# Attention output turned by VectorE in 32 by 32 blocks, and put together by the reload, in place of TensorE transposes

## The chip, the cores and the metric

The kernel runs on one core of one Trainium2 chip. The metric is the device time of one execution in microseconds (us), and the median of the runs is compared. A core has five engines that run their own instruction lists side by side: TensorE (PE, matmuls, with its weight loads as PEld), VectorE (DVE), ScalarE (ACT), GpSimd (POOL) and SyncE (SP), which here issues the DMA transfers, in the order of its list. Engines wait for each other by semaphores. On-chip tiles have 128 partitions (rows of SBUF); PSUM holds the results of PE.

## The reference

One layer of a bidirectional hybrid encoder, for 1024 tokens of width 1024, in float32. What bears on the change:

```python
h = rmsnorm(x, norm_mix)
q, k, v, r, lr_f, lr_b, u, g_a, g_b = split(h @ w_in)      # one wide projection
# 4 heads of 128 key and 256 value columns, chunks of the sequence, both directions
o = o_fwd + o_bwd
o = o * rsqrt(mean(o * o, axis=-1) + 1e-6)                   # per token and head
o = o.transpose(0, 2, 1, 3).reshape(1, 1024, 1024) * gla_norm
o = o * silu(r)
y_a = o @ w_branch_gla
# y_b: pooled mixer of u; merged = sigmoid(g_a) * y_a + sigmoid(g_b) * y_b
x = x + merged @ w_out
# then a SwiGLU feed-forward block with a residual, and a last rmsnorm
```

The attention output `o` comes out with tokens on the partitions. The gate `r` is computed with its columns on the partitions and tokens along the free axis. The product `o * silu(r)` needs both in one layout, the second, and that is where the change sits.

## The kernel before, in words

**Precision.** Matmuls take each float32 operand as a rounded high part and a remainder, and make three products (high x high, low x high, high x low). ACT makes the high part (`wh`, `trh`; helper line L200, or L718), and VectorE or GpSimd subtracts it for the low part (`wl`, `trl`; L201, L709). So a weight that comes from HBM passes DMA, then ACT, then GpSimd, before PE can use it. All matmuls are recorded at one line, L279.

**Stages.** The q and k columns of the projection are made by PE with the attention of the four heads woven in between, from about 130 to 310 us. After the last of them stands a loop over six columns of `r`, 128 wide each: `for j in range(KT - 2)` (L1223; KT is 8). Column j takes its weights (`raw`, two loads of 256 KB at L208, issued ahead), and for each of two halves of 512 tokens runs 24 matmuls (`feature_major`). The r columns 0 to 2 are put aside; from j = 3 on, each half first handles one that was put aside (`put_by`) and then its own, both by `gated`.

**`gated(j, half, src)`** (L1193 on). ACT computes Silu of the r half into `sr` (L1196). PE turns four 128x128 pieces of the attention output `o_heads` into a PSUM bank `tp` (L1199). VectorE multiplies `tp`, `sr` and the norm's factor into a tile `o` (L1206). When two columns are done, both halves are stored to `ob_out` (at a later step, by `flush`, L574). Columns 6 and 7 of r come out of the first gate unit below and pass `gated` there.

**Gate units.** After the loop, pairs of columns are computed together by a scheme of seven products in place of eight (`Gates.run`). Unit 0 holds r columns 6 and 7 and runs products 1, 2, 6, 5, 3, 7. Its weights are `fraw` (512 KB per column, L1096), from which VectorE makes sums `fs` (L1104). Product 1 and 2 use tiles that are on the chip. Product 6 is the first that uses a sum of blocks of the activations: such sums were written to HBM earlier (`f_out`), are loaded into `hs` (L684), and become `trh` on ACT (L718) and `trl` on VectorE (L709). Product 6 also needs a PSUM bank that ACT empties by a copy into `ga` (L1492). There are three `hs` tiles in turn, so a load of `hs` waits for the `trl` of the one three before it. On ACT, the casts `trh`, the Silus, the casts `wh` and the copies `ga` stand in one list.

**The attention output's way.** A head's output is held in two tiles `o` of 128x1024: half of the tokens each, 4 groups of 128 tokens by 256 value columns. `normalize` (L1030) scales the eight groups by 1/rms on VectorE. For heads 0 to 2 both tiles are then stored to `o_out` in HBM (L574), and `load_o` brings them back as `ol` at j = 2, 3 and 4 of the loop (L1044, two loads of 512 KB a head). Head 3, which ends right before column j = 3's first transposes, stays in SBUF.

**What sets the order.** The program is written out by generators: `pump` moves the attention's steps on beside PE's matmuls, `beside` moves the `hs` loads and casts on, `soon` puts a step off by a number of steps. What results is a fixed list for each engine. SP's list is one line for all loads and stores above: an instruction in it that waits holds up all behind it. Eight semaphores serve SP's transfers in rotation, so a transfer also waits for the landing of the one eight places before it.

Of the kernel before, what the change touches and what calls it, by code (L numbers as in the profile page):

```python
# [10 lines left out]
F32 = mybir.dt.float32  # L11
# [4 lines left out]
ALU = mybir.AluOpType  # L16

P = 128
# [3 lines left out]
NT = SEQ // P  # L22
HALF = 512
HEADS = 4
DK = 128
DV = 256
RANK = 16
CH = 128
SUB = 64
GROUPS = 4  # L30
WINDOWS = (2, 4, 8, 16)
# [22 lines left out]
def kernel(  # L54
# [20 lines left out]
    nc = tc.nc  # L75
# [10 lines left out]
    ps_g = ctx.enter_context(tc.tile_pool(name="ps_g", bufs=8 - MM_BANKS, space=bass.MemoryType.PSUM))  # L86

    dram = ctx.enter_context(tc.tile_pool(name="dram", bufs=1, space=bass.MemoryType.DRAM))
# [4 lines left out]
    def name(s):  # L93
        count[0] += 1
        return f"{s}_{count[0]}"

    def slot(dtype=F32, shape=(2, HALF), s="slot"):
        return slots.tile([P, *shape], dtype, tag="slot", name=name(s))

    def t2(width=HALF, dtype=F32, s="t"):  # L100
        return tmp.tile([P, width], dtype, tag="t2", name=name(s), padded_shape=[P, HALF + 2 * PAD])
# [4 lines left out]
    def vec(width, s="v"):  # L106
        return small.tile([P, width], F32, tag="vec", name=name(s), bufs=12)

    def bank(pool, s="ps"):
        return pool.tile([P, HALF], F32, tag=pool.name, name=name(s))  # L110
# [5 lines left out]
    ident = const.tile([P, P], F32, tag="ident", name="ident")  # L116
# [8 lines left out]
    keep = const.tile([P, 4, P], U8, tag="keep", name="keep")  # L125
    carry = const.tile([P, HALF // SUB, SUB], BF16, tag="carry", name="carry")

# [26 lines left out]
    def soon(delay, *steps):  # L154
        put_off.extend([delay, step] for step in steps)
# [36 lines left out]
    def finish_side():  # L192
        while side:
            for _ in side[0][0]:
                pass
            side.pop(0)
# [61 lines left out]
    def take(ahead=True):  # L258

        if not ready:  # L260
            prepare()
        w = ready.pop(0)
        w.finish()
        if ahead:
            prepare()
        return w
# [3 lines left out]
    def halves(ap):  # L270
        return ap.rearrange("p (a c) -> p a c", a=2)

    def sorted_(ap):

        return ap.rearrange("p (c a) -> p a c", a=2)
# [37 lines left out]
    def rms_scale(ms, width, s):  # L313
        rs = vec(width, s)
        nc.vector.tensor_scalar(rs[:, :], ms, EPS, None, op0=ALU.add)
        nc.gpsimd.tensor_tensor(rs[:, :], rs[:, :], half_neg[:, :width], op=ALU.pow)
        return rs
# [132 lines left out]
    g_mix, g_ffn, g_gla, g_pool = (cols[:, 8 * i : 8 * i + 8] for i in range(4))  # L450
    b_dec = (cols[:, 32:36], cols[:, 36:40])
    HALVES = slice(0, HALF), slice(HALF, D)
# [116 lines left out]
    def later(dst, src):  # L569
        deferred.append((dst, src))  # L570
# [105 lines left out]
    def feature_parts():  # L676
        todo = [(p, c) for p in (6, 5, 7, 4) for c in range(2)]
        wholes = []

        def load_sum():  # L680
            if len(wholes) < len(todo):
                p, c = todo[len(wholes)]
                wholes.append(slot(s="hs"))
                nc.sync.dma_start(wholes[-1][:, :, :], f_out[p][:, c])  # L684

        yield load_sum, None, None
        for n, (p, c) in enumerate(todo):
            yield load_sum, wholes[n][:, :, :], p
# [46 lines left out]
    def prepare_beside(jobs, every, put=PUT, lag=1):  # L735
        aside.append([beside(chain(*jobs), every, put, lag), every])

    def finish_beside():
        while aside:
            for _ in aside[0][0]:  # L740
                pass
            aside.pop(0)


    o_heads, unscaled = {}, []
# [78 lines left out]
    def attention(h):  # L824
# [28 lines left out]
        def decay(half, d):  # L853
# [3 lines left out]
            tot = vec(8, "tot")  # L857
            cs3 = cs.rearrange("p (n c) -> p n c", c=SUB)
            la3 = la.rearrange("p (n c) -> p n c", c=SUB)
            cy = carry.rearrange("p n c -> p (n c)")  # L860
            if d == 0:
                nc.vector.tensor_tensor_scan(cs[:, :], cy, la[:, :], 0.0, op0=ALU.mult, op1=ALU.add)
                nc.vector.tensor_copy(tot[:, :], cs3[:, :, SUB - 1])
            else:
# [4 lines left out]
                )  # L869
                nc.vector.tensor_tensor(tot[:, :], cs3[:, :, SUB - 1], la3[:, :, SUB - 1], op=ALU.add)  # L870
            first = cs.rearrange("p (n a c) -> p n a c", a=2, c=SUB)[:, :, 0, :]
            tot2 = tot.rearrange("p (n a) -> p n a", a=2)
# [31 lines left out]
        def chunk_of(e, n, d):  # L904
            return e[n // 4][:, d, (n % 4) * CH : (n % 4 + 1) * CH]

# [28 lines left out]
        def scores(half):  # L935
            sc = [bank(ps_g, "sc") for _ in range(2)]
            for d in range(2):
                for i in range(4):
                    n = 4 * half + i
                    nc.tensor.matmul(  # L940
                        sc[d][:, i * CH : (i + 1) * CH], chunk_of(ke, n, d), chunk_of(qe, n, d),
                        start=True, stop=True,
                    )
            hi, lo = (t2(dtype=F32R, s="p")[:, :] for _ in range(2))
            nc.vector.copy_predicated(sc[1][:, :], keep.rearrange("p n c -> p (n c)"), sc[0][:, :])
            split_to(hi, lo, sc[1][:, :])
            return hi, lo
# [41 lines left out]
        p = scores(0)  # L989
# [3 lines left out]
        o = [slot(shape=(4, DV), s="o") for _ in range(2)]  # L993
        ms = vec(NT, "oms")
        old = sf = None
        for n in range(NT):
            half, i = n // 4, n % 4
# [22 lines left out]
            if n == 3:  # L1020
                p = q_next
            yield 1.02
        rs = rms_scale(ms[:, :], NT, "ors")
        if h == HEADS - 1:
            o_heads[h] = o

        def normalize():
            for n in range(NT):
                t = o[n // 4][:, n % 4, :]
                nc.vector.tensor_scalar(t, t, rs[:, n : n + 1], None, op0=ALU.mult)  # L1030
            if h < HEADS - 1:
                for half in range(2):
                    later(o_out[h][:, 4 * half : 4 * half + 4, :], o[half][:, :, :])

        unscaled.append(normalize)
        if h == HEADS - 1:
            unscaled.pop()()

    o_out = [dram.tile([P, NT, DV], F32, name=f"o_out{h}") for h in range(HEADS - 1)]

    def load_o(h):
        o_heads[h] = [slot(shape=(4, DV), s="ol") for _ in range(2)]
        for half in range(2):
            nc.sync.dma_start(o_heads[h][half][:, :, :], o_out[h][:, 4 * half : 4 * half + 4, :])  # L1044

    def sums_behind():
        prepare_beside(map(feature_sums, range(2)), 2)
# [145 lines left out]
    def gated(j, half, src):  # L1193

        sr = t2(s="sr")
        nc.scalar.activation(halves(sr[:, :]), src, AF.Silu)  # L1196
        tp = bank(ps_g, "tp")
        for i in range(4):
            nc.tensor.transpose(  # L1199
                tp[:, i * P : (i + 1) * P],  # L1200
                o_heads[j // 2][half][:, i, (j % 2) * P : (j % 2 + 1) * P], ident[:, :],
            )
        if j // 2 not in oT:
            oT[j // 2] = [slot(s="o") for _ in range(2)], []
        tiles, there = oT[j // 2]
        nc.vector.scalar_tensor_tensor(  # L1206
            tiles[half][:, j % 2, :], tp[:, :], g_gla[:, j : j + 1], sr[:, :], op0=ALU.mult, op1=ALU.mult
        )
        there.append((j, half))
        if len(there) == 4:  # L1210
            c = j // 2 % 2
            for half, t in enumerate(tiles):
                later(ob_out[j // 4, half][:, 2 * c : 2 * c + 2, :], t[:, :, :])
            soon(2, flush)
# [6 lines left out]
    BY = 3  # L1221
    sums_begun = False
    for j in range(KT - 2):  # L1223
        if 2 <= j <= 4:
            load_o(j - 2)
        w = take()
        if j == 4:
            for _ in range(2):
                gunits[0].load()
        if j == 5:  # L1230
            gates_ahead.step()
        if j < BY:
            whole_r = slot(s="r")
        for half in range(2):
            if j >= BY and not sums_begun and (j > BY or not side):
                finish_side()
                finish_beside()
                prepare_beside([feature_parts()], 5)
                sums_begun = True
            ps = feature_major(w, hT, half)  # L1240
            if half == 0:
                flush()
            elif j == KT - 3:
                for _ in range(2):
                    gunits[1].load()
            if j < BY:
                nc.scalar.copy(halves(whole_r[:, half, :]), sorted_(ps[:, :]))
                raw_r.append((j, half, halves(whole_r[:, half, :])))
            else:
                put_by()  # L1250
                gated(j, half, sorted_(ps[:, :]))
            if j == KT - 3 and half == 0:
                gates_ahead.step()
# [833 lines left out]
    for at, p in enumerate(OUT_ORDER):  # L2087
# [9 lines left out]
        for i in range(CLOSE if closing else n_of):  # L2097
            n = at * n_of + i
# [57 lines left out]
```

## Time and profile before

| | us |
|---|---|
| median of 3 runs (lowest to highest) | 1325.27 (1325.08 to 1325.62) |
| the profiled execution | 1323.53 |
| its span, first to last instruction | 1321.8 |
| PE busy | 1302.2 (99% of the span) |
| VectorE busy | 838.3 (63%) |
| ACT busy | 645.3 (49%) |
| GpSimd busy | 769.0 (58%) |
| transposes at L1199 | 64, from 310.9 to 370.6 |
| stores to `o_out` at L574 | 6, from 131.3 to 257.6 |
| reloads at L1044 | 6, from 260.7 to 302.3 |

Rows of the profile start with a time from the span's start where they come from the timeline (start, length, engine, line, operation, tile written <- tiles read, shape, and in brackets how long the engine was idle before and what released it). Rows by line give the count, the shortest, median and longest duration in ns, and the first and last start. Matmuls overlap on PE, so the distance of their starts is their cost, not their length. For SP, "SPq" marks the issue of a transfer, not the transfer; rows named DMA count the packets that moved in a window of time.

### The profile page before, as it was taken

Reading aid. Unit: us, or ns where it says so; the run is one execution under the profiler, and the core shown is the slowest. Engines: PE = TensorE matmul, PEld = TensorE weight load, DVE = VectorE, ACT = ScalarE, POOL = GpSimd, SP = SyncE. Lnnn points to the kernel's source line nnn. Section 1 sums busy time; section 2 is a strip of 40 time slices with the busy share of each in tenths; the row PEclk is TensorE's granted clock in tenths of the full one; section 3 lists DMA queues with packets and bytes.
Section 4 is the critical chain, followed back from the end, with each engine's and each line's share of the span. In section 5 each row is a group of like instructions: output and inputs, shape, how many; then the busy total and the mean of one; then the engine's idle time right before and its main releaser. Section 6 shows DMA issues by size and latency. Waiting matters only on the chain. (4 is left out here: it accounts for less than half of the span.)

```text
span 1321.8 us, 17901 instructions
## 1 busy us (share of the span) xinstructions
PE 1302.2 (99%) x6310; PEld 1138.0 (86%) x6310; DVE 838.3 (63%) x1034; ACT 645.3 (49%) x1177; POOL 769.0 (58%) x557
## 2 busy tenths in 40 slices
PE   9999999999999999999999999999999999999998
PEld 7888888899888888888888888888888888888886
DVE  6975556554735876778884856566666657354375
ACT  7366766665534545554347633333333334454353
POOL 3332734132598657669675286777766778465454
PEclk9999999999999999999999999999999999999999
DMA  7231623134778678996516355555444457995562
GB/s 236 104 104 42 198 75 117 59 101 128 239 247 283 195 223 303 380 409 212 185 65 240 127 189 186 183 183 173 155 142 159 150 160 257 382 349 201 182 223 80
DMA packets 167835, 251.97 MB, mean 191 GB/s; under 512 B 11161, under 2 KB 94145, under 8 KB 167745
## 3 DMA queue, kind: packets, MB, share of 16 engines
q1 hardware_dynamic: 167600, 250.57, 55.8%
q8 instruction: 49, 0.80, 0.3%
q14 instruction: 42, 0.34, 0.1%
q10 hardware_dynamic: 144, 0.26, 0.1%
HBM read 168.74 MB, written 82.05 MB: 190 GB/s over the span
## 5 line engine op out<-in xcount | busy, mean ns | idle before, releaser
L201 POOL TENSOR_TENSOR wl<-fs,wh 128x512 fp32r<-128x512 f32 x124 | 190.7, 1543 | 138.8 <-ACT wh L200 80.9
L279 PE MATMUL ps<-gh,wh 128*128 128x512 f32 x616 | 234.4, 381 | 0.5 <-DVE sums L1880 0.3
L279 PE MATMUL ps<-gl,wh 128*128 128x512 f32 x616 | 233.6, 379 | 0.7 <-DVE gl L1713 0.7
L279 PE MATMUL ps<-gh,wl 128*128 128x512 f32 x616 | 233.5, 379 | 0.0
L201 POOL TENSOR_TENSOR wl<-fraw,wh 128x512 fp32r<-128x512 f32 x93 | 131.1, 1410 | 58.0 <-ACT wh L200 52.8
L201 POOL TENSOR_TENSOR ol<-gor,oh 128x1024 fp32r<-128x1024 f32 (+1 forms) x42 | 103.2, 2462 | 76.0 <-ACT oh L200 63.1
L279 PE MATMUL ps<-hh,wh 128*128 128x512 f32 x356 | 141.1, 396 | 0.7 <-ACT ga L1492 0.7
L279 PE MATMUL ps<-hh,wl 128*128 128x512 f32 x356 | 134.9, 379 | 0.0
L279 PE MATMUL ps<-hl,wh 128*128 128x512 f32 x356 | 134.9, 379 | 0.0
L279 PEld LDWEIGHTS ps<-gh,wh 128*128 128x128 f32 x616 | 116.5, 189 | 17.9 <-DVE sums L1880 0.7
L279 PEld LDWEIGHTS ps<-gl,wh 128*128 128x128 f32 x616 | 116.4, 189 | 17.4 <-DVE gl L1713 1.1
L279 PEld LDWEIGHTS ps<-gh,wl 128*128 128x128 f32 x616 | 116.4, 189 | 16.5
L279 PE MATMUL ps<-oh,oh 128*128 128x512 f32 x308 | 116.8, 379 | 0.2 <-DVE g L1886 0.2
L279 PE MATMUL ps<-ol,oh 128*128 128x512 f32 x308 | 116.7, 379 | 0.0
L279 PE MATMUL ps<-oh,ol 128*128 128x512 f32 x308 | 116.7, 379 | 0.0
L201 POOL TENSOR_TENSOR wl<-wraw,wh 128x512 fp32r<-128x512 f32 x56 | 91.4, 1663 | 38.3 <-ACT wh L200 36.2
L201 POOL TENSOR_TENSOR wl<-raw,wh 128x512 fp32r<-128x512 f32 x34 | 47.0, 1392 | 103.2 <-ACT wh L200 70.3
L201 DVE TENSOR_TENSOR ol<-wor,oh 128x1024 fp32r<-128x1024 f32 (+1 forms) x42 | 66.6, 1601 | 62.6 <-ACT oh L200 55.1
L200 ACT CAST wh<-fs 128x512 fp32r<-128x512 f32 x124 | 75.8, 612 | 25.7 <-DVE fs L1104 23.8
L279 PEld LDWEIGHTS ps<-hh,wl 128*128 128x128 f32 x356 | 67.3, 189 | 9.6
L279 PEld LDWEIGHTS ps<-hh,wh 128*128 128x128 f32 x356 | 67.4, 189 | 9.3 <-ACT ga L1492 1.1
L279 PEld LDWEIGHTS ps<-hl,wh 128*128 128x128 f32 x356 | 67.4, 189 | 8.4
(281 smaller groups left out, 3059.4 us busy)
## 6 DMA issues: line engine op xcount, KB each, us to landing
fraw<-in_w_ffn_in_dram SPq DMA_DIRECT2D x44, 512.0 KB, 5.9
gor<-g_out SPq DMA_DIRECT2D x35, 512.0 KB, 5.7
fraw<-in_w_in_dram SPq DMA_DIRECT2D x22, 512.0 KB, 6.1
g_out<-s SPq DMA_DIRECT2D x44, 256.0 KB, 2.4
wor<-t_out SPq DMA_DIRECT2D x20, 512.0 KB, 4.2
raw<-in_w_in_dram SPq DMA_DIRECT2D x36, 256.0 KB, 5.2
g_out<-g SPq DMA_DIRECT2D x33, 256.0 KB, 2.6
x<-in_x_dram SPq DMA_DIRECT2D x16, 512.0 KB, 5.2
```

Of the source, the lines that this page charges most:

```text
L200: nc.scalar.copy(hi, src)
L201: eng.tensor_tensor(lo, src, as_f32(hi), op=ALU.subtract)
L279: nc.tensor.matmul(ps.rearrange("p (c a) -> p c a", a=2), a, b.rearrange("p (a c) -> p c a", a=2), **flags)
```

## The change: how heads are turned

The transposes on PE go. VectorE turns each 32x32 block of a head's tile in place, right after the normalisation of that half. All four heads are stored to `o_out` now, head 3 too, half by half. A block turned by itself has its columns on the right rows within 32, but lies in the wrong place of the 128x128 piece. The reload puts it right: for each of the two value columns groups of a head, four DMAs gather 32 value columns of all tokens onto 32 partitions, in pieces of 32 floats (128 bytes). A head's reload is 8 DMAs of 32x32x32 elements in place of 2 of 128x1024, and it now runs for j = 2 to 5. `gated` reads the result straight from SBUF.

```diff
+TB = 32
...
-        if h == HEADS - 1:
-            o_heads[h] = o
 
         def normalize():
-            for n in range(NT):
-                t = o[n // 4][:, n % 4, :]
-                nc.vector.tensor_scalar(t, t, rs[:, n : n + 1], None, op0=ALU.mult)
-            if h < HEADS - 1:
-                for half in range(2):
-                    later(o_out[h][:, 4 * half : 4 * half + 4, :], o[half][:, :, :])
+            for half, t in enumerate(o):
+                for i in range(4):
+                    n = 4 * half + i
+                    nc.vector.tensor_scalar(t[:, i, :], t[:, i, :], rs[:, n : n + 1], None, op0=ALU.mult)
+                turn_blocks(t[:, :, :].rearrange("p n c -> p (n c)"))
+                later(o_out[h][:, 4 * half : 4 * half + 4, :], t[:, :, :])
...
-    o_out = [dram.tile([P, NT, DV], F32, name=f"o_out{h}") for h in range(HEADS - 1)]
+    o_out = [dram.tile([P, NT, DV], F32, name=f"o_out{h}") for h in range(HEADS)]
+
+    def turn_blocks(ap, src=None):
+        nc.vector.transpose(ap, ap if src is None else src)
 
     def load_o(h):
-        o_heads[h] = [slot(shape=(4, DV), s="ol") for _ in range(2)]
-        for half in range(2):
-            nc.sync.dma_start(o_heads[h][half][:, :, :], o_out[h][:, 4 * half : 4 * half + 4, :])
+
+        for i in range(2):
+            t = slot(shape=(NT, P // TB, TB), s="ol")
+            for b in range(P // TB):
+                c = i * P + b * TB
+                nc.sync.dma_start(
+                    t[b * TB : (b + 1) * TB, :, :, :],
+                    o_out[h][:, :, c : c + TB].rearrange("(a p) n c -> p n a c", p=TB),
+                )
+            o_heads[2 * h + i] = t[:, :, :, :].rearrange("p n a c -> p (n a c)")
...
-        tp = bank(ps_g, "tp")
-        for i in range(4):
-            nc.tensor.transpose(
-                tp[:, i * P : (i + 1) * P],
-                o_heads[j // 2][half][:, i, (j % 2) * P : (j % 2 + 1) * P], ident[:, :],
-            )
...
-            tiles[half][:, j % 2, :], tp[:, :], g_gla[:, j : j + 1], sr[:, :], op0=ALU.mult, op1=ALU.mult
+            tiles[half][:, j % 2, :], o_heads[j][:, HALVES[half]], g_gla[:, j : j + 1], sr[:, :], op0=ALU.mult, op1=ALU.mult
...
     for j in range(KT - 2):
-        if 2 <= j <= 4:
+        if 2 <= j <= 5:
             load_o(j - 2)
```

The engines' lists move as follows. Lines are those of each kernel's own file, and numbers after a name tell apart the tiles of one name.

First VectorE, from the 1/rms of head 3 to the first gated products, before the change:

```order
L315 TENSOR_SCALAR ors_3302<-oms_3103 128x8
L1030 TENSOR_SCALAR o_3101<-o_3101,ors_3302 128x256 x4
L1030 TENSOR_SCALAR o_3102<-o_3102,ors_3302 128x256 x4
L1206 SCALAR_TENSOR_TENSOR o_3320<-tp_3315,cols,sr_3313 128x512
L1206 SCALAR_TENSOR_TENSOR o_3330<-tp_3325,cols,sr_3323 128x512
```

and with it:

```order
L316 TENSOR_SCALAR ors_3321<-oms_3116 128x8
L1030 TENSOR_SCALAR o_3114<-o_3114,ors_3321 128x256 x4
L1041 STREAM_TRANSPOSE o_3114<-o_3114 128x1024
L1030 TENSOR_SCALAR o_3115<-o_3115,ors_3321 128x256 x4
L1041 STREAM_TRANSPOSE o_3115<-o_3115 128x1024
L1209 SCALAR_TENSOR_TENSOR o_3338<-ol_2968,cols,sr_3336 128x512
L1209 SCALAR_TENSOR_TENSOR o_3343<-ol_3169,cols,sr_3341 128x512
```

Two turns of head 3 stand between its normalisation and the gated products, which read the reloaded tiles `ol` in place of PSUM.

Second SP, from the first `hs` (for product 6) through j = 4 and its weights, before:

```order
L684 DMA hs_3349<-f_out_563 128x1024
L1044 DMA ol_3376<-o_out_567 128x1024
L1044 DMA ol_3377<-o_out_567 128x1024
L208 DMA raw_3380<-in_w_in_dram 128x4x128
L208 DMA raw_3382<-in_w_in_dram 128x4x128
L1096 DMA fraw_3384<-in_w_in_dram 128x8x128
L1096 DMA fraw_3386<-in_w_in_dram 128x8x128
L684 DMA hs_3415<-f_out_563 128x1024
L684 DMA hs_3423<-f_out_562 128x1024
```

and with the change:

```order
L575 DMA o_out_568<-o_3114 128x1024
L575 DMA o_out_568<-o_3115 128x1024
L685 DMA hs_3362<-f_out_563 128x1024
L1049 DMA ol_3379<-o_out_567 32x32x32 x4
L1049 DMA ol_3384<-o_out_567 32x32x32 x4
L209 DMA raw_3389<-in_w_in_dram 128x4x128
L209 DMA raw_3391<-in_w_in_dram 128x4x128
L1105 DMA fraw_3393<-in_w_in_dram 128x8x128
L1105 DMA fraw_3395<-in_w_in_dram 128x8x128
L685 DMA hs_3424<-f_out_563 128x1024
L685 DMA hs_3432<-f_out_562 128x1024
```

Head 3's two stores, which need the two turns above, now stand ahead of the `hs` load, of head 2's reload (eight DMAs for two), of the weights `raw` that are for j = 5, and of unit 0's `fraw`.

Third SP, a little later, at the `hs` loads for product 7 (`f_out_564`), before:

```order
L684 DMA hs_3463<-f_out_562 128x1024
L684 DMA hs_3505<-f_out_564 128x1024
L574 DMA ob_out_2740<-o_3320 128x1024
L574 DMA ob_out_2741<-o_3321 128x1024
L684 DMA hs_3528<-f_out_564 128x1024
```

and with the change:

```order
L685 DMA hs_3462<-f_out_562 128x1024
L1049 DMA ol_3482<-o_out_568 32x32x32 x4
L1049 DMA ol_3487<-o_out_568 32x32x32 x4
L685 DMA hs_3504<-f_out_564 128x1024
L575 DMA ob_out_2747<-o_3338 128x1024
L575 DMA ob_out_2748<-o_3339 128x1024
L685 DMA hs_3527<-f_out_564 128x1024
```

Head 3's reload, at j = 5, is new there, ahead of the two `hs` loads for product 7.

## The prediction

> **What bounds the kernel now.** I read the page first, for the engine that is busy all the time, and then the chain of waits, for what it waits on.
>
> ```profile
> PE 1302.2 (99%) x6310; PEld 1138.0 (86%) x6310; DVE 838.3 (63%) x1034; ACT 645.3 (49%) x1177; POOL 769.0 (58%) x557
> ...
> PE 42%; DVE 2%; ACT 1%; issue 1%; DMA 0%; POOLq 0%; POOL 0%; ACTq 0%; DVEq 0%
> ```
>
> PE works for 1302.2 us of the 1321.8 us span. So each matmul that goes is time saved, as long as PE finds its operands ready. A stall of PE is time lost, and nothing later makes it up. DMA has 0% of the chain: at present no transfer is late. The change acts between 250 and 372 us, so I read that stretch engine by engine, first PE by line and along the timeline.
>
> ```profile
> L1199 PE MATMUL tp<-ident,ol x48: 272/273/273, 310.9 to 341.9; 128*128 128x128 f32 x48
> L1199 PE MATMUL tp<-ident,o x16: 272/273/273, 349.9 to 370.6; 128*128 128x128 f32 x16
> ...
> 267.70 0.38 PE L279 MATMUL ps<-hl,wh 128*128 128x512 f32 x1
> ...
> 271.80 0.38 PE L279 MATMUL ps<-hh,wl 128*128 128x512 f32 x1
> ...
> 310.85 1.04 PE L1199 MATMUL tp<-ident,ol 128*128 128x128 f32 x8
> ...
> 316.91 1.04 PE L1199 MATMUL tp<-ident,ol 128*128 128x128 f32 x8
> ...
> 329.81 0.46 PE L279 MATMUL ps<-hh,wh 128*128 128x512 f32 x1
> ...
> 341.93 0.46 PE L279 MATMUL ps<-hh,wh 128*128 128x512 f32 x1
> 347.19 0.46 PE L279 MATMUL ps<-trh,wh 128*128 128x512 f32 x1
> ```
>
> The 64 transposes stand on PE between 310.9 and 370.6. Column j = 5 of the loop starts at 329.81, gate unit 0 at 341.93 and its product 6, the first that reads a combined block `trh`, at 347.19. Matmuls of 512 columns run 0.216 us apart (267.70 to 271.80 in 19 steps).
>
> **What the change removes.** One period of the loop is 316.91 - 310.85 = 6.06 us, of which 24 matmuls take 24 x 0.216 = 5.18 us. The remaining 0.88 us is the price of 8 transposes, 0.11 us each (the 0.27 us of a row overlaps its neighbour). All 64 are worth **7.0 us**. By the start of j = 5, 32 of them are gone (3.5 us, so PE would be there at 326.3); by product 6, 48 (5.3 us, so at 341.9); 16 come later (1.76 us).
>
> **What it adds on VectorE.** Eight block turns of 128x1024. The trace has no such operation.
>
> ```profile
> 135.89 0.69 DVE L855 TENSOR_TENSOR la<-la,z 128x512 f32<-128x512 f32 x1 [2.56 <-ACT z L848]
> ...
> 200.66 0.76 DVE L503 TENSOR_TENSOR vl<-ps,vh 128x256 fp32r<-128x256 f32 x2 [3.02 <-ACT vh L501]
> ...
> 260.63 0.69 DVE L855 TENSOR_TENSOR la<-la,z 128x512 f32<-128x512 f32 x1 [3.04 <-ACT z L848]
> ...
> 313.29 2.19 DVE L1030 TENSOR_SCALAR o<-o,ors 128x256 f32<-128x256 f32 x8 [1.75 <-POOL ors L316]
> L709 DVE TENSOR_TENSOR trl<-hs,trh x8: 1211/1222/2299, 325.0 to 355.0; 128x1024 fp32r<-128x1024 f32 x8
> ```
>
> A normalisation pass handles 128x1024 elements in 2.19 / 2 = 1.10 us; a pass with two inputs over the same shape takes 1.21 to 2.30 us. Those are my bounds for one turn. I take 1.15 us, since a turn has one input, as the normalisation has. For heads 0 to 2 the two turns (2.3 us) fit into the idle 2.56, 3.02 and 3.04 us that follow those normalisations: nothing on the path. At 2.3 us a turn 1.6 to 2.0 us would stick out for each head, on an engine that is idle for over a third of the span. Head 3 has no such gap: its first half is ready at 313.29 + 1.10 + 1.15 = 315.5 and its second at 317.8. The multiplications with the gate (L1206) move 2.3 us later, which PE does not see: PSUM is emptied by the Silu on ACT, and only the stores of `ob_out` wait for VectorE.
>
> **What it adds and moves on the DMA queue.** This is where I put the result.
>
> ```profile
> 288.01 0.34 SPq L684 DMA_DIRECT2D hs<-f_out  x1
> 301.87 0.81 SPq L1044 DMA_DIRECT2D ol<-o_out  x2
> 302.78 0.94 SPq L208 DMA_DIRECT2D raw<-in_w_in_dram  x2
> 303.81 3.72 SPq L1096 DMA_DIRECT2D fraw<-in_w_in_dram  x2
> 308.19 24.97 SPq L684 DMA_DIRECT2D hs<-f_out  x4
> 333.22 0.90 SPq L574 DMA_DIRECT2D ob_out<-o  x2
> 337.02 3.13 SPq L684 DMA_DIRECT2D hs<-f_out  x3
> ...
> DMA to landing us min/median/max: 4.0/4.0/4.0
> ```
>
> SP issues in order. Before the change the weights of j = 5 leave at 302.78, 27 us ahead of their use, and the first `hs` at 288.01. In the new order the two stores of head 3's turned tiles stand ahead of all of these, from `hs` on. They wait for the turns, so they leave at 315.5 and 317.8 and `hs` leaves at 318.2. Behind it follow, in order: the reload of head 2 in eight DMAs, the weights of j = 5 (0.5 MB), two `fraw` (1.05 MB), three `hs` (1.57 MB), the reload of head 3 in eight DMAs, `hs`, two `ob_out`, `hs` (2.1 MB). What left up to 30 us earlier now leaves behind them, so the price of a reload counts.
>
> ```profile
> DMA packets 570, 0.14 MB, mean 284 GB/s; under 512 B 545, under 2 KB 545, under 8 KB 570
> ...
> DMA packets 3306, 2.20 MB, mean 323 GB/s; under 512 B 86, under 2 KB 3158, under 8 KB 3304
> ```
>
> A reload DMA now moves 32x32x32 elements: 1024 pieces of 128 B. Let c be its time on a full queue. The first row is 0.5 us from 15.2 on, when the low-rank weights came in by pieces of 128 B: 545 small packets in 0.5 us, so 0.94 us per 1024. The second is 6.8 us from 306.2 on, mostly 512-byte pieces: 6.8 / 3306 x 1024 = 2.1 us per 1024. These are the bounds; the pieces have the size of the first row's, so I take c = 1.0. A head cost 1.05 MB at 323 GB/s, 3.2 us, and costs 8c = 8 us now.
>
> The Trainium skill, "DMA: Bandwidth & Descriptors", section Specifications, says that a transfer needs at least 512 B for line rate and is done by read-modify-write below it. An estimate that halves the 323 GB/s for that gives 0.81 us for 128 KB, and the change of the sum below would be +10.4 instead of +13.5 us; the 0.94 us of the trace is dearer than this page makes it.
>
> **The sum.** A 512 KB load into an empty queue lands 4.0 us after issue (the landing row of the old reload).
>
> 1. `hs` lands at 318.2 + 4.0 = 322.2. Head 2's reload takes until 322.2 + 8c, the weights of j = 5 until 323.8 + 8c (0.5 MB at 323 GB/s is 1.6 us), and their casts need 1.1 us more:
>
> ```profile
> 317.60 1.13 ACT L200 CAST wh<-raw 128x512 fp32r<-128x512 f32 x2
> ...
> 338.62 1.04 ACT L718 CAST trh<-hs 128x1024 fp32r<-128x1024 f32 x1
> 341.50 1.05 ACT L718 CAST trh<-hs 128x1024 fp32r<-128x1024 f32 x1 [1.83 <-DMA hs<-f_out]
> ...
> 346.53 0.58 ACT L1492 COPY ga<-ps 128x512 f32<-128x512 f32 x1
> ```
>
> PE stands ready at 326.3 and starts at 324.9 + 8c: a **first stall** of 8c - 1.4 = 6.6 us. Queued behind that cast on ACT are the Silus and the `trh` casts, which wait with it.
>
> 2. Product 6 needs a PSUM bank that ACT empties into `ga`. That copy (346.53) stands behind the last two `trh` casts (338.62, 341.50) on ACT, the second of which waited for its `hs`. From that cast's start to the end of the copy it is 347.1 - 341.5 = 5.6 us. In the new order this `hs` lands after 1.05 MB + 0.5 MB + 1.57 MB = 3.1 MB (9.7 us at 323 GB/s), the second reload, and 2.1 MB (6.5 us): 322.2 + 8c + 9.7 + 8c + 6.5 = 338.4 + 16c. Product 6 can start at 344.0 + 16c = 360.0, against 347.1 before: 12.9 us later. The `hs` tiles that the queue waited for before (issues at 333.22 and 337.02) come free while head 3's reload drains, so I add nothing there. PE arrives at 341.9 + 6.6 = 348.5 and waits, a **second stall** of some 10 us that swallows the first.
>
> 3. The clock.
>
> ```profile
> 1316.00:1318.00 2.00, 0.00 (x0) 0.00 (x0) 0.96 (x2) 1.00 (x3) 0.55 (x1) 1.00 0.64 242
> 1318.00:1320.00 2.00, 0.00 (x0) 0.00 (x0) 0.00 (x0) 0.00 (x0) 0.00 (x0) 1.00 0.60 231
> 1320.00:1321.80 1.80, 0.00 (x0) 0.00 (x0) 0.00 (x0) 0.00 (x0) 0.00 (x0) 0.54 0.10 34
> ...
> 1.42 5.06 PE L472 MATMUL warm<-ident 128*128 128x128 f32 x24 [1.42 <-POOL ident masks.py:199]
> ```
>
> At the end of the program the granted clock drops to 0.54 once PE has been idle for over 4 us (no matmul from 1316 on). A stall of 10 us is long enough for that. At the start 24 small matmuls take 5.06 us, 0.21 each where a warm one takes 0.11: getting warm costs half of 5.06, less what fell into full speed. I take 2.3 us, between nothing and 2.5. The Trainium skill, "TensorE: Matmul & The Clock Gate", Part 1, gives a window of about 3.4 us at half speed; an estimate by that is 1.7 us lost and 0.6 us less in the sum.
>
> 4. Sum: +12.9 + 2.3 - 1.76 (the 16 transposes behind this point) = 16c - 2.55 = **+13.5 us**. On the profiled execution's 1323.53 us that is 1337.0. The median of the runs, 1325.27, lies 1.74 above it, so I forecast 1338.8. With c = 0.94 it is +12.5 us.
>
> **The rivals.**
>
> *Only the first stall is left* (the later loads pass, because `hs` and weights drain faster than 323 GB/s beside the small pieces). -7.0 + 6.6 + 2.3 = +1.9 us, 1327.2. For it: the queue's rate is an average over a mix, and ACT's order leaves no slack only at one copy. Against it: with c = 0 the copy would still end at 344.0, after the 341.9 at which PE gets there.
>
> *Faster: the reload is hidden altogether.* Then only the transposes count: -7.0 us, 1318.3. It would need the loads behind head 3's stores to be in time although they leave up to 30 us later; it decides only if the weights of j = 5 land by 325.2, thus c below 0.2 us, a fifth of the lower bound. For it: the tiles it fills are read by VectorE alone, and the 16 DMA engines may drain the pieces beside the large transfers. This is the case on the other side.
>
> *The pieces cost what 512-byte packets cost.* With c = 2.1 the sum is 16 x 2.1 - 2.55 = +31 us, 1356.3. For it: 1024 packets are 1024 packets, and the second row's queue was as full as this one will be. Against it: the first row shows the same piece size at less than half of that.
>
> **How the numbers follow.** The forecast has 0.70, the three rivals 0.10 each. The range should leave out no more than the tails of the first and of the last two: 1326 to 1354. The forecast's own range is 1334 to 1348: a rate a quarter above 323 GB/s takes 3.2 us off the 16.2 us for 5.2 MB, and c = 1.6 adds 9.6 us. A difference of 0.2%, 2.65 us, is about what a measurement here can tell from none. The hidden case is faster: 0.10. The single stall, at +1.9 us, is within that bound, less a little for its spread: 0.09. The rest, 0.81, is slower.
>
> **What would show it.** Right: the transposes gone from PE; in its place an idle stretch before the first matmul of j = 5 (some 7 us, released by the casts of `raw`), and a longer one before product 6, released by ACT's `ga`; SP's `hs` issue near 318 instead of 288, and the granted clock below 1 after each stall; eight reload DMAs draining in about 8 us per head. Wrong: turns far above 1.15 us on VectorE, which would show as idle PE in heads 0 to 2; reload DMAs at 2 us each; or no idle PE at product 6, which would mean that the `trh` casts were not held up.

## The result, and the profile after

| | before | with the change |
|---|---|---|
| median | 1325.17 us (4 runs, 1324.83 to 1325.62) | 1336.63 us (4 runs, 1336.46 to 1338.59) |
| ratio, 95% interval | | 1.0088 [1.0075, 1.0101] |
| profiled execution | 1323.53 us, span 1321.8 | 1336.46 us, span 1334.7 |

The change makes the kernel 11.5 us slower by the medians, and 12.9 us by the profiled executions. The forecast was 1338.8 us, in the range 1326 to 1354.

The page of the changed kernel: engines and the count of DMA packets.

```profile
PE 1301.9 (98%) x6246; PEld 1135.5 (85%) x6246; DVE 850.6 (64%) x1042; ACT 645.7 (48%) x1177; POOL 768.0 (58%) x557
...
DMA packets 200538, 254.07 MB, mean 190 GB/s; under 512 B 44376, under 2 KB 127360, under 8 KB 200448
```

64 matmuls are gone from PE (6310 to 6246), and 33,000 DMA packets below 512 B are new (11,161 to 44,376). PE's busy time hardly fell (1302.2 to 1301.9 us), because PE ran at half clock for a while behind each of two stalls (read below). The loss shows in the waits of PE (the engine and line that waited, the releaser, us in total, times, longest):

```profile
PE ps L280 <- ACT ga L1495: 9.7, 2, 9.0
PE ps L280 <- ACT wh L201: 5.4, 1, 5.4
```

Before the change the first of these was 0.7 us and the second not there. On PE's timeline they stand at the two places of the forecast, the first matmul of column j = 5 and the first of product 6:

```profile
331.93 0.79 PE L280 MATMUL ps<-hh,wh 128*128 128x512 f32 x1 [5.36 <-ACT wh L201]
...
360.33 0.80 PE L280 MATMUL ps<-trh,wh 128*128 128x512 f32 x1 [9.05 <-ACT ga L1495]
```

Product 6 starts at 360.33 in place of 347.19. SP's list shows why:

```profile
282.60 1.48 SPq L209 DMA_DIRECT2D raw<-in_w_in_dram  x2
315.75 2.64 SPq L575 DMA_DIRECT2D o_out<-o  x2
318.48 0.39 SPq L685 DMA_DIRECT2D hs<-f_out  x1
318.96 8.08 SPq L1049 DMA_DIRECT2D ol<-o_out  x8
327.14 1.33 SPq L209 DMA_DIRECT2D raw<-in_w_in_dram  x2
...
330.05 3.31 SPq L685 DMA_DIRECT2D hs<-f_out  x3
333.46 11.08 SPq L1049 DMA_DIRECT2D ol<-o_out  x8
...
346.40 3.09 SPq L685 DMA_DIRECT2D hs<-f_out  x3
```

From 284.1 to 315.75, for over 31 us, SP issues nothing: it stands at the store of head 3's first turned tile, whose turn ends at 315.73. Before, the first `hs` left at 288.01 and the weights of j = 5 at 302.78; they leave at 318.48 and 327.14. What waits for them on ACT:

```profile
331.26 0.62 ACT L201 CAST wh<-raw 128x512 fp32r<-128x512 f32 x1 [14.42 <-DMA raw<-in_w_in_dram]
...
350.08 1.05 ACT L719 CAST trh<-hs 128x1024 fp32r<-128x1024 f32 x1 [5.46 <-DMA hs<-f_out]
354.45 1.04 ACT L719 CAST trh<-hs 128x1024 fp32r<-128x1024 f32 x1 [3.33 <-DMA hs<-f_out]
...
359.70 0.58 ACT L1495 COPY ga<-ps 128x512 f32<-128x512 f32 x1
```

The added work itself is cheap on VectorE, and hidden where the forecast hid it:

```profile
L1041 DVE STREAM_TRANSPOSE o<-o x8: 1245/1246/1247, 131.5 to 316.8; 128x1024 f32<-128x1024 f32 x8
...
260.63 0.69 DVE L856 TENSOR_TENSOR la<-la,z 128x512 f32<-128x512 f32 x1 [0.51 <-ACT z L849]
```

A turn takes 1.25 us. The instruction behind head 2's two turns still starts at 260.63, as before; only its idle time shrank from 3.04 to 0.51 us.

### The profile page after: what moved, and what is told of

It reads as the page before. It is cut to its first block, busy times and chain, and to the rows that moved or that the text cites. A ratio compares the mean times of both kernels' runs of the same rounds, so it can differ in the third digit from the quotient of the medians.

```text
span 1334.7 us, 17804 instructions
## 1 busy us (share of the span) xinstructions
PE 1301.9 (98%) x6246; PEld 1135.5 (85%) x6246; DVE 850.6 (64%) x1042; ACT 645.7 (48%) x1177; POOL 768.0 (58%) x557
## 2 busy tenths in 40 slices
DMA packets 200538, 254.07 MB, mean 190 GB/s; under 512 B 44376, under 2 KB 127360, under 8 KB 200448
## 5 line engine op out<-in xcount | busy, mean ns | idle before, releaser
L280 PEld LDWEIGHTS ps<-hh,wh 128*128 128x128 f32 x356 | 68.1, 191 | 15.6 <-ACT wh L201 5.8
L280 PEld LDWEIGHTS ps<-hh,wl 128*128 128x128 f32 x356 | 67.9, 191 | 10.7 <-POOL wl L202 0.9
L280 PE MATMUL ps<-trh,wh 128*128 128x512 f32 x176 | 68.0, 387 | 9.0 <-ACT ga L1495 9.0
```

Of the source, the lines that this page charges most:

```text
L280: nc.tensor.matmul(ps.rearrange("p (c a) -> p c a", a=2), a, b.rearrange("p (a c) -> p c a", a=2), **flags)
```

## The experiments

All were compared with the kernel before on the same chip as they ran on; "ratio" is to that kernel, with its 95% interval.

### 1. Head 3's stores behind the loads

```diff
-                later(o_out[h][:, 4 * half : 4 * half + 4, :], t[:, :, :])
+                (late_o.append if h == HEADS - 1 else deferred.append)((o_out[h][...], t[:, :, :]))
...
             for _ in range(2):
                 gunits[0].load()
+            store_late()          # at j == 4: issues what late_o holds
```

> The changed kernel with one thing moved: the two stores of head 3's turned tiles are issued at j = 4 behind the two loads for gate unit 0, in place of ahead of the first hs load, head 2's reload and the weights of j = 5. Theory (the two stalls come from the SP list standing still until the turns of head 3 are done, at 315.5 and 317.8 us): the first hs leaves before 300 us again, both stalls are gone, and the 7.0 us of the transposes are left as a gain: 1318 to 1320 us. Rival (the 128-byte pieces are the cause wherever they stand: 8 us a head on the queue): head 2's reload still holds the weights of j = 5 and head 3's the hs for product 7, PE waits before product 6 and the time stays above 1328 us.

Measured: 1326.39 us, ratio 1.0002 [0.9992, 1.0011]. Neither theory fits whole: the time is neither's, and the wait before product 6 that the rival names is there. SP's list, PE's only long wait in this stretch, and the last `hs` cast ahead of the copy that PE waits for:

```profile
288.02 0.34 SPq L685 DMA_DIRECT2D hs<-f_out  x1
301.88 8.26 SPq L1055 DMA_DIRECT2D ol<-o_out  x8
310.24 1.17 SPq L209 DMA_DIRECT2D raw<-in_w_in_dram  x2
...
315.75 2.64 SPq L1047 DMA_DIRECT2D o_out<-o  x2
318.49 3.50 SPq L685 DMA_DIRECT2D hs<-f_out  x3
```

```profile
348.25 0.79 PE L280 MATMUL ps<-trh,wh 128*128 128x512 f32 x1 [6.16 <-ACT ga L1502]
...
342.37 1.04 ACT L719 CAST trh<-hs 128x1024 fp32r<-128x1024 f32 x1 [2.73 <-DMA hs<-f_out]
```

The first stall is gone: the standing SP list caused it. Of the 11.5 us all but 0.9 come back, and the interval does not tell that rest from none. But the 7.0 us of the transposes are not gained. PE reaches product 6 at 342.1, some 5 us sooner than before, waits 6.16 us and starts at 348.25, 1.1 us later than before. Part of that wait is still the change's: the last `hs` is issued behind head 3's reload, and its cast waited 2.73 us for it to land. Whether something that was there before the change also eats the transposes' gain, this run does not tell; experiments 2 and 5 do.

### 2. Head 3 left on PE

```diff
-        if 2 <= j <= 5:
+        if 2 <= j <= 4:
...                # in normalize:
+                if h < HEADS - 1:
                     turn_blocks(...)
                     later(...)
...                # in gated:
+        if j // 2 == HEADS - 1:
+            # tp and four transposes, as before the change
```

> Heads 0 to 2 as in the change (turned on VectorE, 8 reload DMAs a head), head 3 as before: not turned, not stored, 16 transposes on PE. Theory: 48 transposes of 0.11 us are gone and SP never waits for head 3, so 1325.2 - 5.3 = 1320 us, with no idle PE before j = 5 or product 6. Rival (price of the 128-byte pieces of heads 0 to 2 counts by itself): the time is at or above 1325 us.

Measured: 1325.44 us, ratio 0.9993 [0.9983, 1.0003]. Here nothing of the change touches the two stores, and no stall stands before j = 5. Yet 48 transposes are gone for no gain: PE's wait before product 6 is there again, and ACT's list shows what the copy stood behind.

```profile
346.83 0.48 PE L280 MATMUL ps<-trh,wh 128*128 128x512 f32 x1 [3.60 <-ACT ga L1508]
```

```profile
337.86 1.05 ACT L719 CAST trh<-hs 128x1024 fp32r<-128x1024 f32 x1 [0.35 <-DMA hs<-f_out]
...
345.67 0.62 ACT L201 CAST wh<-fs 128x512 fp32r<-128x512 f32 x1 [4.72 <-DVE fs L1116]
346.20 0.58 ACT L1508 COPY ga<-ps 128x512 f32<-128x512 f32 x1
```

`hs` has landed by 337.86 and is not late. The copy waits behind a weight cast, which waits for VectorE.

### 3. The reload in two plain loads

```diff
-            t = slot(shape=(NT, P // TB, TB), s="ol")
-            for b in range(P // TB):
-                ...               # 4 DMAs of 32x32x32
+            t = slot(shape=(4, DV), s="ol")
+            nc.sync.dma_start(t[:, :, :], o_out[h][:, 4 * i : 4 * i + 4, :])
```

> The changed kernel with the reload in two loads of 128x1024 a head, as the stored tiles lie, in the same places of the SP list; what it leaves out is that the 32x32 blocks are put to their rows. Turns, stores and order stay. Theory (both count: the plug delays everything, and the price of the reload behind it is added twice): 3.2 us a head in place of 8, so the sum 16c - 2.55 with 8c = 3.2 gives +3.9 us, 1329 us; the first stall near 2 us, product 6 some 3 us later than before. Rival A (only the wait for head 3's turns matters, the loads drain beside it): unchanged at 1336 us. Rival B (only the pieces matter): the gain of the transposes shows, 1318 us.

Measured: 1330.96 us, ratio 1.0035 [1.0022, 1.0047].

```profile
329.14 0.48 PE L280 MATMUL ps<-hh,wh 128*128 128x512 f32 x1 [2.25 <-ACT wh L201]
...
352.38 0.79 PE L280 MATMUL ps<-trh,wh 128*128 128x512 f32 x1 [4.83 <-ACT ga L1490]
```

The stalls are 2.25 us (near 2 expected) and at product 6, which starts 5.2 us later than before (3 expected). Both rivals fall: about half of the loss goes with the small pieces (5.7 of 11.5 us), and about half stays with the order, that is with head 3's stores ahead of the loads and its reload, now plain, behind them.

### 4. Head 3's reload behind the loop

```diff
-        if 2 <= j <= 5:
+        if 2 <= j <= 4:
             load_o(j - 2)
...                # after the loop over j:
+    load_o(HEADS - 1)
```

> The changed kernel with head 3's reload moved behind the loop, that is behind the two hs loads for product 7 and the loads for gate unit 1; head 3's stores stay where the change has them. Theory: the first stall stays at 5.4 us, the hs for product 7 land 7 us sooner, product 6 starts near 353 in place of 360, and the time is 1330 to 1332 us, unless head 3's reload now comes too late for its multiplication with the gate, which would hold the casts behind it on VectorE. Rival (head 3's reload drains beside the others and costs nothing on the path): unchanged at 1336 us.

Measured: 1335.47 us, ratio 1.0070 [1.0051, 1.0089].

```profile
355.73 0.48 PE L280 MATMUL ps<-trh,wh 128*128 128x512 f32 x1 [3.87 <-ACT ga L1496]
...
365.21 0.48 PE L280 MATMUL ps<-hh,wh 128*128 128x512 f32 x1 [2.35 <-ACT ga L1496]
```

Product 6 starts 4.6 us sooner than with the change, so head 3's reload did stand in its way, though for less than the 7 us expected. The time hardly follows. Product 3 now waits 2.35 us where it waited 0.68 with the change, and the granted clock falls again behind that wait (0.58 from 366 to 368 us, 0.57 in the two after). Another 1.7 us goes near 670 us (the last section), so the two profiled executions end within 0.3 us of each other. The expectation had named a wait there, with a reload that lands too late as its cause. The profile doesn't show that: VectorE's last wait for a transfer ahead of the gate's product ends at 359.2, and the product starts at 360.90, released by ACT. PE waits for a copy on ACT that itself waited for a `trl` on VectorE; why it needs that one was not tested.

### 5. The transposes left out, nothing else

Experiments 1 and 2 point to a wait of the kernel before. This run puts it to the test by itself.

```diff
-        tp = bank(ps_g, "tp")
-        for i in range(4):
-            nc.tensor.transpose(...)
...
-            tiles[half][:, j % 2, :], tp[:, :], g_gla[:, j : j + 1], sr[:, :], ...
+            tiles[half][:, j % 2, :], o_heads[j // 2][half][:, 2 * (j % 2) : 2 * (j % 2) + 2, :], ...
```

> The kernel before with nothing changed but that the 64 transposes and their PSUM bank are left out: the gate multiplies the attention output as it lies, untransposed, which leaves out the turning of that output altogether. Theory after the first four runs (the gain of the 48 transposes ahead of product 6 can't be had, because product 6 waits for ACT's copy ga, which had no slack before; PE idles there for over 3 us and runs at half clock afterwards): 5.3 us are lost again, 1.76 are gained behind, some 2.5 us go to the clock: 1324 to 1327 us, with idle PE of 3 to 5 us before product 6. Rival (each transpose that goes is time won): 1325.4 - 7.0 = 1318.4 us.

Measured: 1323.85 us, ratio 0.9989 [0.9980, 0.9997]. Of 7.0 us of removed PE work 1.1 us are gained (the kernel before had 1324.91 us beside it). PE's wait, and the stretch around it (columns: length, busy us and count of PE, PEld, DVE, ACT, POOL, then granted clock, DMA share, GB/s):

```profile
346.09 0.80 PE L279 MATMUL ps<-trh,wh 128*128 128x512 f32 x1 [3.90 <-ACT ga L1486]
```

```profile
344.00:346.00 2.00, 0.00 (x0) 0.00 (x0) 2.00 (x3) 1.07 (x3) 0.72 (x2) 0.95 1.13 339
346.00:348.00 2.00, 1.91 (x5) 1.55 (x6) 1.65 (x3) 2.00 (x5) 2.00 (x2) 0.50 1.03 419
348.00:350.00 2.00, 2.00 (x8) 1.65 (x7) 0.85 (x1) 1.50 (x3) 2.00 (x2) 0.70 0.98 397
```

PE starts product 6 only 1.1 us sooner than before, and at half clock, which takes 1.5 us. With the 16 transposes behind that point (1.76 us) this leaves 1.1 - 1.5 + 1.76 = 1.4 us, near what was measured: the 48 ahead of it win nothing.

### 6. ACT's copy ahead of the weight cast, alone

```diff
+            if n == 0 and at == 0:
+                zs[of].run(p)             # product 1, with its copy ga
+                gates_ahead.step()        # the next weight cast
```

> The kernel before with one thing moved: in gate unit 0, ACT's copy ga of product 1 stands ahead of the next weight cast wh<-fs, which waits for VectorE, in place of behind it. A control for the two runs after it. Theory: before, PE reached product 6 at the moment at which the copy was done, so an earlier copy wins nothing: 1325 us, within 1 us. Rival (the copy held PE before, too): faster by more than 2 us.

Measured: 1325.69 us, ratio 1.0003 [0.9994, 1.0013]: no difference, as the theory has it.

### 7. Head 3 on PE, and the copy moved

The edits of 2 and 6 together.

> Heads 0 to 2 turned and reloaded as in the change, head 3 by 16 transposes on PE, and the copy ga of product 1 moved ahead of the weight cast. Theory (the lost gain sat in that wait on ACT): product 6 starts near 343.5 in place of 346.8, the idle PE before it and the half clock behind it are gone, and the 48 transposes show: 1320 to 1321 us. Rival (the gain is lost elsewhere, to DMA or VectorE): 1325 us as without the move.

Measured: 1323.17 us, ratio 0.9983 [0.9974, 0.9992]. The wait before product 6 is gone, so that was the place. Another follows at product 3, and the clock falls to half after it:

```profile
350.73 0.48 PE L280 MATMUL ps<-hh,wh 128*128 128x512 f32 x1 [2.53 <-ACT ga L1508]
```

```profile
350.00:352.00 2.00, 1.27 (x4) 1.09 (x5) 0.64 (x1) 0.68 (x2) 2.00 (x3) 0.80 0.21 84
352.00:354.00 2.00, 2.00 (x6) 1.55 (x6) 2.00 (x3) 0.62 (x1) 0.67 (x2) 0.50 0.00 0
```

Product 3 still starts 3.0 us sooner than before; the half clock takes 1.7 us of that back. It is the fastest of all kernels here that compute the whole layer, and better than both kernels of this case, by 0.17% and 1.0%, but the gain is a third of the 5.3 us of its 48 transposes.

### 8. All 64, with three moves

Edits 1 and 6, and `load_o(HEADS - 1)` moved to the second half of j = 5, ahead of the loads for gate unit 1.

> The change with three moves: head 3's stores behind the loads for gate unit 0 (as in the first run), head 3's reload behind the hs loads for products 7 and 4 and ahead of the loads for gate unit 1, and the copy ga of product 1 ahead of the weight cast. Theory: no stall of more than 1 us is left and all 64 transposes are won: 1318 to 1320 us. Rival A (hs for product 7 still arrives late because head 3's stores hold the SP list until 318): product 6 waits some 3 us and half clock follows, 1323 to 1326 us. Rival B (head 3's reload lands too late for its product with the gate): a wait shows at product 3.

Measured: 1328.96 us, ratio 1.0031 [1.0019, 1.0043]. A miss: the wait of Rival A came, and behind it a wait at product 3.

```profile
345.46 0.76 PE L280 MATMUL ps<-trh,wh 128*128 128x512 f32 x1 [2.96 <-ACT ga L1503]
...
357.85 0.79 PE L280 MATMUL ps<-hh,wh 128*128 128x512 f32 x1 [5.25 <-ACT ga L1503]
```

```profile
354.05 0.62 ACT L201 CAST wh<-fraw 128x512 fp32r<-128x512 f32 x1 [1.52 <-DMA fraw<-in_w_in_dram]
...
357.21 0.58 ACT L1503 COPY ga<-ps 128x512 f32<-128x512 f32 x1 [2.55 <-DMA ob_out<-o]
```

Product 3 waits for ACT's copy, and ACT waits for `fraw` and for stores of `ob_out`, which all stand behind head 3's reload on SP now. That is not Rival B's reason: head 3's product with the gate waits for GpSimd there and not for the reload. None of the three places tried for that reload (j = 5, here, behind the loop) leaves PE without a wait.

### 9. Head 3's transfers on ACT's queue

Edits 1 and 6, with `nc.scalar.dma_start` for head 3's stores and reload.

> The change with head 3's two stores (at j = 4) and its eight reload DMAs (at j = 5) issued by ACT in place of SP, and the copy ga of product 1 ahead of the weight cast. SP's list is then as before but for head 2's eight DMAs. Theory (SP's waiting list made the first hs and the weights late, not the traffic itself): hs leave near 288 and 310 again, product 6 starts within 1 us of the 342.4 of the run before with head 3 on PE, and with the last 16 transposes gone too the time is 1321 to 1323 us; a short wait at product 3 stays. Rival (the 16 DMA engines, or ACT's own time for issuing eight DMAs at 0.7 us each, are the limit): PE waits before product 6 for over 3 us and the time is at or above 1325 us.

Measured: 1334.12 us, ratio 1.0058 [1.0041, 1.0076]. The rival's time and its second form hold:

```profile
332.96 10.66 ACTq L1055 DMA_DIRECT2D ol<-o_out  x6
343.66 0.62 ACT L201 CAST wh<-fraw 128x512 fp32r<-128x512 f32 x1 [10.94 <-issue]
```

Issuing six of these DMAs holds ACT for 10.7 us, and the weight cast behind them makes PE wait 7.06 us at gate unit 0. Nor did SP's list stay free: its last two reload DMAs of head 2 left at 319.3 and 319.9, after head 3's stores. The waits of SP tell why: the first of the two waited 11.9 us for one of these stores, with which it shares one of the eight semaphores. So this run doesn't test the theory by itself, since the stores still held SP's list.

### 10. The copies of products 6 and 5 moved, too

Edit 7 with `at < 4` in place of `at == 0`.

> As the run with head 3 on PE and the copy of product 1 moved (1323.2 us), with the copies of products 6 and 5 moved ahead of the weight casts as well. Theory (what is left there is PE's idle 2.5 us before product 3, again behind the copy ga on ACT, and half clock behind it): product 3 starts near 348.5 in place of 350.7, and the time is 1320 to 1322 us. Rival: the weight casts that now come later make PE wait instead, and the time is 1323 us or more.

Measured: 1325.92 us, ratio 1.0004 [0.9993, 1.0014]. The theory missed: product 3 starts at 353.18, after a wait of 4.79 us for ACT's `ga`, in place of 2.53. The copy that product 3 needs is itself kept waiting now, by GpSimd's low part of a weight whose cast came later:

```profile
352.54 0.59 ACT L1508 COPY ga<-ps 128x512 f32<-128x512 f32 x1 [2.74 <-POOL wl L202]
```

Between 335 and 355 us VectorE is busy for 18.4 of the 20 us, and ACT (12.3) and GpSimd (13.3) wait for it and for each other in turn; here, moving one instruction forward moved another back.

### 11. The reload in pieces of half the size

```diff
-                nc.sync.dma_start(t[b * TB : (b + 1) * TB, :, :, :], o_out[h][:, :, c : c + TB]...)
+                for e in (0, TB // 2):
+                    nc.sync.dma_start(t[..., e : e + TB // 2], o_out[h][:, :, c + e : c + e + TB // 2]...)
```

> The changed kernel with each reload DMA split in two of 32x32x16 elements: the same bytes in twice as many pieces, of 64 B. Theory (the price of a reload goes by pieces, 0.93 us per 1024 as the trace of the change has it, and stands twice in the path of product 6): head 2's and head 3's reload take some 15 us each in place of 7.4 and 6.7, product 6 starts 14 us later than 360.3, and the time is 1350 us (within 3). Rival A (the price goes by bytes): unchanged at 1336.6 us. Rival B (a fixed time for each of the now 16 DMAs, by the 0.4 us of a plain issue): 3 to 6 us later, 1340 to 1343 us.

Measured: 1349.85 us, ratio 1.0190 [1.0173, 1.0207].

```profile
337.38 0.80 PE L280 MATMUL ps<-hh,wh 128*128 128x512 f32 x1 [10.11 <-ACT wh L201]
...
371.04 0.80 PE L280 MATMUL ps<-trh,wh 128*128 128x512 f32 x1 [15.65 <-ACT ga L1496]
```

```profile
DMA packets 14598, 1.01 MB, mean 92 GB/s; under 512 B 14420, under 2 KB 14597, under 8 KB 14597
```

The same bytes in twice as many pieces cost more, and more than Rival B's 3 to 6 us: both rivals fall. Product 6 starts 10.7 us later than with the change, not 14: the row covers 11.0 us from 324.3 on, so 0.77 us per 1024 pieces of 64 B. The time came out as expected in part by another loss: this profiled execution ran at half clock near 685 us as well (the last section).

## Why the prediction was right, step by step

**The two stalls and their sum held.** With c = 1.0 the forecast had PE start j = 5 at 332.9 and product 6 at 360.0; measured 331.93 and 360.33. Its wait before product 6 was to be some 10 us (9.05), the last `hs` to land at 354.4 (its cast began at 354.45), SP to be free of head 3's stores at 318.2 (318.48). A full queue moved this:

```profile
DMA packets 6303, 0.98 MB, mean 163 GB/s; under 512 B 5820, under 2 KB 6303, under 8 KB 6303
```

That is 6.0 us from 324.2 on: 6.0 / 6303 x 1024 = 0.97 us per 1024 packets, at the lower bound and not the upper. The first stall was 1.2 us shorter than forecast. One cost of it was left out: the granted clock was at half behind it, too (0.50 from 332 to 338 us), so PE reached product 6 at 351.28 and not at 348.5. Nothing hung on either, because the second wait ended when ACT's copy was done, whenever PE came. Experiments 1, 3, 4 and 11 take away or enlarge one part each of the sum: the standing list (first stall gone), the pieces (about half of the loss), head 3's reload (4.6 us at product 6), the count of pieces (+10.7 us). All moved product 6 the way that 16c and the fixed part say; the sizes agree less well, as with the 4.6 us of head 3's reload, which stands in the sum with 8c.

**The turn** measured 1.25 us, against 1.15 taken within 1.10 to 2.30, and was hidden for heads 0 to 2.

**The clock.** The table of windows of the changed kernel after product 6 starts:

```profile
360.00:362.00 2.00, 1.67 (x4) 1.40 (x5) 2.00 (x2) 1.43 (x3) 2.00 (x3) 0.50 1.02 418
362.00:364.00 2.00, 2.00 (x6) 1.55 (x6) 2.00 (x3) 1.87 (x3) 2.00 (x1) 0.50 0.82 334
364.00:366.00 2.00, 2.00 (x7) 1.61 (x6) 1.25 (x1) 0.78 (x3) 2.00 (x2) 0.53 0.05 18
```

Half clock from 360.3 to near 365.8. The lag behind the kernel before grows from 13.1 us at product 6 to 15.6 us at its last matmul: 2.4 us, against 2.3 forecast. The Trainium skill, "TensorE: Matmul & The Clock Gate", Part 1, gives about 3.4 us at half clock; by an estimate from that figure 1.7 us would be lost. Here it was 5.5 us, and the measurement decides.

**The offset.** The profiled executions differ by 12.93 us (forecast 13.5), the medians by 11.46. The forecast added the 1.74 us between median and profiled execution of before, and after the change that offset was 0.2 us. That makes 1.6 of the 2.2 us between 1338.8 and 1336.63; the other 0.6 us is the sum. The last section shows where such an offset can come from. Nothing in the change makes it; without it the forecast would have been 1337.0.

**What was wrong: the gain.** The forecast booked 7.0 us for the transposes and worked out the hidden case as -7.0 us, 1318.3. Its own sum used the right value without saying so (5.3 us of it end in the wait at product 6, and only 1.76 us are subtracted), but the rival priced the full removal. Experiment 5 gives 1.1 us. ACT's copy `ga` ended at 347.11 and product 6 began at 347.19: that row, quoted in the prediction, already said that PE had no slack to win there. The first rival (+1.9 us, one stall) carried the same error, since it booked -7.0, too. For the faster case the condition on c was also wrong: in experiments 1, 2 and 5 the weights of j = 5 come in time, and the time still doesn't reach it.

**The chances.** At 1336.63 us the time fell into the forecast's own case, 1334 to 1348.

## What to carry to other kernels

An instruction that is added to an in-order DMA list costs first what stands behind it: ask when its data will be ready, and which loads were leaving early only because the list was free. A saving on the busiest engine is worth only what lies behind the next point at which that engine already arrives just in time; look for a wait of 0 to 1 us there before the saving is booked, and remember that idling at that point can cost the clock. Price a scatter or gather by its pieces and not by its bytes: 1 MB in 128-byte pieces took 7 to 8 us here, and 3.2 us would have been its time at the rate of large pieces.

## What the runs showed of the hardware

**A short idle time of PE is enough for half clock.** In experiment 7 the granted clock fell to 0.50 after PE had waited 2.53 us, in experiment 2 after 3.60 us, and there once more near 163 us after 2.00 us. The wait of 0.68 us before product 3 in the kernel before left it at 1.00.

**It comes in some executions and not in others.** Far behind the change, near 657 us, PE runs through several waits of 0.3 to 1.4 us for weights. The kernel before (first fence) and experiment 6 (second fence), which does the same work there:

```profile
658.00:660.00 2.00, 1.67 (x8) 1.16 (x7) 2.00 (x4) 2.00 (x4) 2.00 (x2) 1.00 0.00 0
660.00:662.00 2.00, 2.00 (x11) 1.73 (x11) 2.00 (x1) 1.12 (x2) 2.00 (x2) 1.00 0.00 0
```

```profile
658.00:660.00 2.00, 1.68 (x6) 1.07 (x6) 2.00 (x4) 2.00 (x5) 2.00 (x2) 0.80 0.00 0
660.00:662.00 2.00, 2.00 (x6) 1.53 (x6) 2.00 (x2) 1.01 (x2) 2.00 (x2) 0.50 0.00 0
```

The second is 1.7 us later against the first behind that stretch than ahead of it. Experiments 4, 7, 10 and 11 lose as much at that place, the profiled execution of the change nothing, though all do the same work there. So an execution of one and the same kernel may well be 1.7 us longer, which is near the offset of 1.74 us between the profiled execution of before and its median. The other executions have no trace that would show the place, but their mean granted clock is on record: of the kernel before, 41 executions at 0.999 or 1.000 took 1324.8 us in the mean, and 33 at 0.996 to 0.998 took 1326.2.

**The price of 1024 pieces** was 0.97 us for 128 B and 0.77 us for 64 B on a full queue. The Trainium skill, "DMA: Bandwidth & Descriptors", section Specifications, has read-modify-write below 512 B; an estimate that halves the rate of 323 GB/s for it gives 0.81 and 0.41 us. The runs show a price that follows the count of pieces more than the bytes.

**Issuing costs its engine.** The issue of a reload DMA with 1024 pieces took 0.56 to 4.0 us, 0.79 in the median, where one of 128x1024 took 0.40. On SP it did not show, as SP issues nothing but transfers; on ACT it held the casts back (experiment 9).
